# Half-row adds on GpSimd, and whole-load row sums, in a log-sum-exp kernel

## The chip, the cores and the metric

The kernel runs on one core of one Trainium2 chip. The metric is the device time of one execution in microseconds; "before" stands at a median of 162.42 us over 3 runs (162.29 to 162.43). The engines that matter are ScalarE (ACT, exponentials and logarithms), VectorE (DVE, sums), GpSimd (POOL), SyncE (SP, whose queue issues the transfers) and the 16 DMA engines. TensorE (PE) only adds up a check.

## The reference

For each of 32 x 512 = 16384 rows of 1024 float32 values, the reference gives one float32:

```python
max_x = np.max(x, axis=-1, keepdims=True)
return max_x.squeeze(-1) + np.log(np.sum(np.exp(x - max_x), axis=-1))
```

The input is drawn from a standard normal distribution, 67.1 MB in all, and each value is read once.

## The kernel before

**Tiling.** The rows are spread over 128 partitions, 128 rows per partition; a "row" below is one such column of 128 rows, 1024 values on each partition, and `c` counts them. Columns 0 to 111 (`W` = 112) and 112 to 127 are stored apart. The kernel takes exp(x) without subtracting the maximum, sums it, and takes the logarithm. A check of the sums (too small, too large, not a number) ends in one value, `fine`; only if it fails does a second pass with the maximum run, which does not happen with this input.

**Loads.** The list `LOADS` (L17) cuts the 128 rows into 18 transfers, numbered 0 to 17 here: sizes in rows, shrinking towards the end. SP issues all of them (L126) in that order into a ring of 48 rows in SBUF. A load that overwrites ring space waits first for whoever read it last (`users`, L119 to 126): SP's queue is in order, so a load that waits holds those behind it back. Load 3 starts again at ring row 0, and load 6 as well.

**What is done with a load** is written beside its size, one letter and a count of rows at a time. ScalarE waits for the landing once for the load, then works in place:

- `R`: one exponential over the rows (L192), then one VectorE row sum over them (L196).
- `T`: one exponential (L192), then for each row one VectorE instruction that adds the two halves of the row and sums the result (L204).
- `A`: ScalarE's exponential sums its row as it goes (L181); one row each.
- `Y`, `Z`: the two pieces of the last row, each summed by ScalarE (L170).

The last exponential of a load also covers what has landed of the row after.

**Order.** Each engine runs its instructions in the order in which this loop writes them. Waits between engines are counters (`Counted`), each wait naming how far another engine must have come. When `c` reaches `LATE` = 119, after the T3 of load 10, ScalarE gets the logarithm of columns 0 to 111 (L219), which waits for the VectorE instruction noted in `early_sum`, the last one that wrote these columns; VectorE gets the early check (L133, L138). After the loop come the store of these columns (L227), the logarithms of the remaining columns (L230, L232), their store (L236), the late check (L242) and `fine` (L251). GpSimd does nothing in the loop.

Of the kernel before, what the change touches and what calls it, by code (L numbers as in the profile page):

```python
# [13 lines left out]

LOADS = [  # L17
# [4 lines left out]
]  # L22


# [23 lines left out]
def kernel(  # L48
# [5 lines left out]
    nc = tc.nc  # L54
# [8 lines left out]
    AX = mybir.AxisListType  # L63
    ALU = mybir.AluOpType

    x_flat = x.flatten_outer_dims()
    n, d = x_flat.shape
    assert n % P == 0
    NC = n // P
    H = d // 2  # L70
    W = NC - B
# [7 lines left out]
    def source(e0, size):  # L79
        assert e0 >= W * d or e0 + size <= W * d  # L80
        return x_rest[:, e0 - W * d : e0 - W * d + size] if e0 >= W * d else x_rows[:, e0 : e0 + size]

    loads = [
        (int(size * d), [(op[0], 0 if op[0] == "Y" else int(op[1:] or 1)) for op in ops.split()])
        for size, ops in LOADS
    ]
# [3 lines left out]
    def sbuf(name, cols, dtype=fp32, rows=P):  # L90
        return nc.alloc_sbuf_tensor(name, [rows, cols], dtype).ap()

    ring = sbuf("ring", RING * d)
    sumexp = sbuf("sumexp", NC + 1)
# [10 lines left out]
    act = Counted(nc, nc.scalar, "act")  # L105
    dve = Counted(nc, nc.vector, "dve")
    pe = Counted(nc, nc.tensor, "pe")
    sp = Counted(nc, nc.sync, "early_store")
    done = nc.alloc_semaphore("done")
    again = nc.alloc_semaphore("again")  # L110
# [8 lines left out]
    users = []  # L119

    def load(i, here, done_before, size):
        for a, b, who, at in users:
            if a < here + size and b > here:
                sp.wait(who, at)
        users[:] = [u for u in users if not (u[0] < here + size and u[1] > here)]
        return nc.sync.dma_start(  # L126
            out=ring[:, here : here + size], in_=source(done_before, size)
        ).then_inc(landed[i], 16)

    def check_early():  # L130
        dve.wait(act, summed_by_act)
        dve.wait(dve, dve.n)
        dve.did(nc.vector.tensor_scalar(  # L133
            out=clamped[:, 0:LATE], in0=sumexp[:, 0:LATE],
            scalar1=LOW, scalar2=HIGH, op0=ALU.max, op1=ALU.min,
        ))
        dve.wait(dve, dve.n)
        dve.did(nc.vector.scalar_tensor_tensor(  # L138
            out=clamped[:, 0:LATE], in0=clamped[:, 0:LATE], scalar=0.0, in1=sumexp[:, 0:LATE],
            op0=ALU.bypass, op1=ALU.not_equal, accum_out=bad[:, 0:1],  # L140
        ))
        pe.wait(dve, dve.n)
        pe.did(nc.tensor.matmul(count, lhsT=bad[:, 0:1], rhs=far, start=True, stop=False))  # L143

    def add_up(c, who, **kw):
        pe.wait(*who)
        return pe.did(nc.tensor.matmul(count, lhsT=ones, rhs=sumexp[:, c : c + 1], **kw))  # L147

    c = 0
    p = 0  # L150
    here = 0
    done_before = 0
    summed_by_act = 0
    ln_early = None
    first_load = None
    for i, (size, ops) in enumerate(loads):
        if here + size > RING * d:
            assert here == p
            p = here = 0
        dma = load(i, here, done_before, size)  # L160
        first_load = first_load or dma.ins
        end = here + size
        done_before += size
        act.wait(landed[i], 16)
        for k, (how, s) in enumerate(ops):
            rows = ring[:, p : p + s * d].rearrange("p (c d) -> p c d", d=d)
            if how in "YZ":

                assert c == LAST and (how == "Z" or here == p)
                at = act.did(nc.scalar.activation(  # L170
                    out=last_exp[:, here - p : end - p], in_=ring[:, here:end], func=AF.Exp,
                    accum_out=sumexp[:, LAST : NC] if how == "Y" else sumexp[:, NC : NC + 1],
                ))
                here = end
                if how == "Y":
                    first_piece = at
                summed_by_act = at
            elif how == "A":
                assert here == p
                v = ring[:, p : p + d]  # L180
                at = act.did(nc.scalar.activation(  # L181
                    out=v, in_=v, func=AF.Exp, accum_out=sumexp[:, c : c + 1]
                ))
                here += d
                users.append((p, p + d, act, at))
                summed_by_act = at
                who = (act, at)
            else:

                upto = end if k + 1 == len(ops) and c + s < LAST else p + s * d  # L190
                v = ring[:, here:upto]
                at = act.did(nc.scalar.activation(out=v, in_=v, func=AF.Exp))  # L192
                here = upto
            if how == "R":
                dve.wait(act, at)
                who = (dve, dve.did(nc.vector.reduce_sum(  # L196
                    out=sumexp[:, c : c + s], in_=rows, axis=AX.X
                )))
                users.append((p, p + s * d, *who))
            elif how == "T":  # L200
                dve.wait(act, at)
                for r in range(s):
                    lo = rows[:, r, 0:H]
                    who = (dve, dve.did(nc.vector.scalar_tensor_tensor(  # L204
                        out=lo, in0=lo, scalar=1.0, in1=rows[:, r, H:d],
                        op0=ALU.mult, op1=ALU.add, accum_out=sumexp[:, c + r : c + r + 1],
                    )))
                    users.append((p + r * d, p + (r + 1) * d, *who))
                    if c + r >= LATE:
                        add_up(c + r, who, start=False, stop=False)  # L210
            if how == "A" and c >= LATE:
                add_up(c, who, start=False, stop=False)
            c += s
            p += s * d
            if c == LATE:

                act.wait(dve, early_sum)
                act.wait(act, early_act)
                ln_early = act.did(nc.scalar.activation(  # L219
                    out=res[:, 0:W], in_=sumexp[:, 0:W], func=AF.Ln  # L220
                ))
                check_early()
            if c <= W:
                early_sum, early_act = dve.n, summed_by_act
        assert here == end
    sp.wait(act, ln_early)
    nc.sync.dma_start(out=out_rows, in_=res[:, 0:W]).then_inc(sp.sem, 16)  # L227
# [5 lines left out]
        out=res[:, LAST:NC], in_=sumexp[:, NC : NC + 1], func=AF.Ln, bias=sumexp[:, LAST:NC]  # L233
# [9 lines left out]
        out=clamped[:, LATE:NC], in0=sumexp[:, LATE:NC], scalar=LOW,  # L243
        in1=sumexp[:, LATE:NC], op0=ALU.max, op1=ALU.not_equal, accum_out=bad[:, 1:2],
# [4 lines left out]
    at = add_up(NC, (act, summed_by_act), start=False, stop=True)  # L249
    dve.wait(pe, at)  # L250
    at = dve.did(nc.vector.tensor_scalar(out=fine, in0=count, scalar1=HIGH, scalar2=None, op0=ALU.is_lt))  # L251
# [6 lines left out]
    with nc.If(all_fine < 1):  # L258
# [3 lines left out]
        rows = 0  # L262
        steps = 0
        for c0 in range(0, NC, RING):
            s = min(RING, NC - c0)
# [5 lines left out]
            for c1, c2 in ((c0, edge), (edge, c0 + s)):  # L271
                if c1 == c2:
                    continue
                nc.scalar.dma_start(
                    out=ring[:, (c1 - c0) * d : (c2 - c0) * d],
                    in_=source(c1 * d, (c2 - c1) * d),
# [4 lines left out]
                out=neg, in_=v, op=ALU.max, axis=AX.X, negate=True  # L281
# [3 lines left out]
                out=v, in0=v, in1=neg[:, :, None].to_broadcast([P, s, d])  # L285
# [5 lines left out]
                out=sumexp[:, c0 : c0 + s], in_=v, axis=AX.X  # L291
# [71 lines left out]
```

## Time and profile before

| what | value |
|---|---|
| median of 3 runs | 162.42 us |
| the profiled execution, its own time | 162.54 us |
| its span, first to last instruction | 161.2 us |
| VectorE busy | 120.4 us (75%) |
| ScalarE busy | 116.2 us (72%) |
| GpSimd busy | 0.2 us (four memsets before the loop) |
| read from HBM | 67.11 MB, 417 GB/s over the span |
| transfers of the loads | 97.3% of the 16 DMA engines' span |
| VectorE's row sums, `R` | 15 instructions, 108.8 us |
| VectorE's half-row add and sum, `T` | 17 instructions, 10.7 us |
| ScalarE's summing exponentials, `A` | 9 instructions, 9.4 us |

The profile is of one execution; all places in time are microseconds from the start of its span. A busy share is an average: which engine sets the time is read stage by stage. A transfer has an issue on SP's queue and a time from issue to landing. When several transfers are queued, the time to landing includes the wait behind those ahead. An instruction on one engine can begin slightly before the one ahead has ended in the records, so durations in a row add up to a little more than the stretch they take: exponentials start some 0.09 us, row sums 0.08 us before the one ahead ends.

### The profile page before, as it was taken

Reading aid. Unit: us, or ns where it says so; the run is one execution under the profiler, and the core shown is the slowest. Engines: PE = TensorE matmul, PEld = TensorE weight load, DVE = VectorE, ACT = ScalarE, POOL = GpSimd, SP = SyncE. Lnnn points to the kernel's source line nnn. Section 1 sums busy time; section 2 is a strip of 40 time slices with the busy share of each in tenths; the row PEclk is TensorE's granted clock in tenths of the full one; section 3 lists DMA queues with packets and bytes.
Section 4 is the critical chain, followed back from the end, with each engine's and each line's share of the span. In section 5 each row is a group of like instructions: output and inputs, shape, how many; then the busy total and the mean of one; then the engine's idle time right before and its main releaser. Section 6 shows DMA issues by size and latency. Waiting matters only on the chain.

```text
span 161.2 us, 227 instructions
## 1 busy us (share of the span) xinstructions
PE 2.1 (1%) x24; PEld 1.0 (1%) x24; DVE 120.4 (75%) x57; ACT 116.2 (72%) x49; POOL 0.2 (0%) x4
## 2 busy tenths in 40 slices
PE   0000000000000000000000000000000000000022
PEld 0000000000000000000000000000000000000011
DVE  0000000009999999999999999999999995999894
ACT  3000059990799709995199949983999999989995
POOL 0000000000000000000000000000000000000000
DMA  7996996996996996996999999997999999999991
GB/s 260 520 520 276 504 520 276 504 520 276 504 520 276 504 520 276 504 520 276 463 439 439 439 423 407 445 534 331 439 439 419 434 407 430 442 419 410 410 397 25
DMA packets 2883, 67.19 MB, mean 417 GB/s; under 512 B 577, under 2 KB 705, under 8 KB 1345
## 3 DMA queue, kind: packets, MB, share of 16 engines
q1 hardware_dynamic: 2880, 67.18, 97.3%
q14 instruction: 3, 0.02, 0.0%
HBM read 67.11 MB, written 0.07 MB: 417 GB/s over the span
## 4 chain that ended last, share of the span: by engine, by line
DVE 51%; DMA 29%; ACT 16%; issue 2%; PE 0%
DVE sumexp L196 51%; DMA ring<-in_x_dram 29%; ACT ring L192 15%; ACT last_exp L170 1%; ACT res L219 0%; PE count L147 0%; DVE fine L251 0%
## 5 line engine op out<-in xcount | busy, mean ns | idle before, releaser
L196 DVE TENSOR_REDUCE sumexp<-ring 128x8 f32<-128x8192 f32 (+6 forms) x15 | 108.8, 7326 | 36.3 <-ACT ring L192 36.3
L192 ACT ACTIVATE ring<-ring 128x8192 f32<-128x8192 f32 (+15 forms) x23 | 103.8, 4571 | 41.8 <-DMA ring<-in_x_dram 41.8
L204 DVE SCALAR_TENSOR_TENSOR ring<-ring 128x512 f32<-128x512 f32 x17 | 10.7, 689 | 0.6 <-ACT ring L192 0.6
L181 ACT ACTIVATE ring<-ring 128x1024 f32<-128x1024 f32 x9 | 9.4, 1041 | 0.0
L114 ACT ACT_TABLE_LOAD x1 | 1.3, 1283 | 1.5 <-PEq L57 1.5
L143 PE MATMUL count<-far,bad 128*1 128x1 f32 x2 | 0.2, 164 | 153.7 <-DVE clamped L138 153.7
L147 PE MATMUL count<-sumexp,ones 128*1 128x1 f32 x20 | 1.8, 164 | 3.5 <-DVE ring L204 3.4
L181 ACT ACTIVATION_READ_ACCUMULATOR ring<-ring 128x1 f32 x9 | 1.7, 186 | 0.0
L204 DVE DVE_READ_ACCUMULATOR ring<-ring 128x1 f32 x17 | 1.4, 83 | 0.0
L115 DVE MEMSET ones<- 128x1 f32 x1 | 0.1, 59 | 1.5 <-PEq L57 1.5
L170 ACT ACTIVATE last_exp<-ring 128x640 f32<-128x640 f32 (+1 forms) x2 | 1.2, 591 | 0.0
L143 PEld LDWEIGHTS count<-far,bad 128*1 128x1 f32 x2 | 0.1, 80 | 153.7 <-DVE clamped L138 153.7
L147 PEld LDWEIGHTS count<-sumexp,ones 128*1 128x1 f32 x20 | 0.8, 81 | 4.4 <-DVE ring L204 4.2
L251 DVE TENSOR_SCALAR fine<-count 1x1 int32<-1x1 f32 x1 | 0.1, 147 | 0.6 <-PE count L147 0.6
L170 ACT ACTIVATION_READ_ACCUMULATOR last_exp<-ring 128x1 f32 x2 | 0.4, 186 | 0.0
L138 DVE SCALAR_TENSOR_TENSOR clamped<-clamped,sumexp 128x119 f32<-128x119 f32 x1 | 0.3, 284 | 0.0
L232 ACT ACTIVATE res<-sumexp 128x1 f32<-128x1 f32 x1 | 0.3, 294 | 0.0
L219 ACT ACTIVATE res<-sumexp 128x112 f32<-128x112 f32 x1 | 0.3, 279 | 0.0
L242 DVE SCALAR_TENSOR_TENSOR clamped<-sumexp 128x9 f32<-128x9 f32 x1 | 0.2, 169 | 0.1
L133 DVE TENSOR_SCALAR clamped<-sumexp 128x119 f32<-128x119 f32 x1 | 0.2, 222 | 0.0
L230 ACT ACTIVATE res<-sumexp 128x15 f32<-128x15 f32 x1 | 0.2, 198 | 0.0
L248 PE MATMUL count<-far,bad 128*1 128x1 f32 x2 | 0.2, 164 | 0.0
(8 smaller groups left out, 0.7 us busy)
## 6 DMA issues: line engine op xcount, KB each, us to landing
ring<-in_x_dram SPq DMA_DIRECT2D x1, 6912.0 KB, 26.0
ring<-in_x_dram SPq DMA_DIRECT2D x1, 6400.0 KB, 23.9
ring<-in_x_dram SPq DMA_DIRECT2D x1, 4608.0 KB, 17.7
ring<-in_x_dram SPq DMA_DIRECT2D x1, 3840.0 KB, 19.3
ring<-in_x_dram SPq DMA_DIRECT2D x1, 2816.0 KB, 25.6
ring<-in_x_dram SPq DMA_DIRECT2D x1, 2368.0 KB, 25.2
ring<-in_x_dram SPq DMA_DIRECT2D x1, 1696.0 KB, 21.7
ring<-in_x_dram SPq DMA_DIRECT2D x1, 1248.0 KB, 24.4
```

The costliest lines, as they stand in the source:

```text
L114: nc.scalar.preload_act_table_set("natural_log_exp_and_others")
L133: dve.did(nc.vector.tensor_scalar(out=clamped[:, 0:LATE], in0=sumexp[:, 0:LATE], scalar1=LOW, scalar2=HIGH, op0=ALU.max, op1=ALU.min,))
L138: dve.did(nc.vector.scalar_tensor_tensor(out=clamped[:, 0:LATE], in0=clamped[:, 0:LATE], scalar=0.0, in1=sumexp[:, 0:LATE], op0=ALU.bypass ...
L143: pe.did(nc.tensor.matmul(count, lhsT=bad[:, 0:1], rhs=far, start=True, stop=False))
L147: return pe.did(nc.tensor.matmul(count, lhsT=ones, rhs=sumexp[:, c : c + 1], **kw))
L170: at = act.did(nc.scalar.activation(out=last_exp[:, here - p : end - p], in_=ring[:, here:end], func=AF.Exp, accum_out=sumexp[:, LAST : NC ...
L181: at = act.did(nc.scalar.activation(out=v, in_=v, func=AF.Exp, accum_out=sumexp[:, c : c + 1]))
L192: at = act.did(nc.scalar.activation(out=v, in_=v, func=AF.Exp))
L196: who = (dve, dve.did(nc.vector.reduce_sum(out=sumexp[:, c : c + s], in_=rows, axis=AX.X)))
L204: who = (dve, dve.did(nc.vector.scalar_tensor_tensor(out=lo, in0=lo, scalar=1.0, in1=rows[:, r, H:d], op0=ALU.mult, op1=ALU.add, accum_out ...
L219: ln_early = act.did(nc.scalar.activation(out=res[:, 0:W], in_=sumexp[:, 0:W], func=AF.Ln))
L232: ln_last = act.did(nc.scalar.activation(out=res[:, LAST:NC], in_=sumexp[:, NC : NC + 1], func=AF.Ln, bias=sumexp[:, LAST:NC]))
```

## The change

A new letter, `F`: one exponential over the rows as in `R`; then GpSimd adds the second half of each row onto its first half, one `tensor_tensor` for all rows of the piece; then VectorE sums the half rows, one row sum over 512 values per row. VectorE's part is not written at once: it is kept in `folded`, and `reduce_folded` writes it when the next `F` begins, after the VectorE work of the next `R` or `T`, or before a load that would overwrite the rows. 35 rows are done this way, in seven pieces of 9, 6, 6, 4, 4, 3 and 3 rows in loads 3 to 8. No row is summed by ScalarE's `A` any more. Loads 1 and 2 are one piece of 16 rows each, as load 0 was (before: two of 8). Sizes and order of the loads, and loads 9 to 17, are as they were. In load 4 the piece that VectorE sums whole is now the second. Of the 35 rows, 29 were `R` before, 4 were `A` and 2 were `T`; the other five `A` rows become `R`.

```diff
 LOADS = [
-    (16, "R16"), (16, "R8 R8"), (16, "R8 R8"), (16, "R8 R8"), (13.5, "R7 R6"),
-    (12.5, "R7 R6"), (9, "A A A A A A A A A"), (7.5, "R3 R2 R2"), (5.5, "R4 T2"),
-    (4.625, "T4"), (3.3125, "T3"), (2.4375, "T3"), (1.8125, "T2"), (1.3125, "T1"), (0.9375, "T1"),
-    (0.5625, "T1"), (0.625, "Y"), (0.375, "Z"),
+    (16, "R16"), (16, "R16"), (16, "R16"), (16, "F9 R7"), (13.5, "F6 R7"), (12.5, "R7 F6"),
+    (9, "R5 F4"), (7.5, "F4 R3"), (5.5, "F3 F3"), (4.625, "T4"), (3.3125, "T3"), (2.4375, "T3"),
+    (1.8125, "T2"), (1.3125, "T1"), (0.9375, "T1"), (0.5625, "T1"), (0.625, "Y"), (0.375, "Z"),
 ]
...
+    folded = []
+
+    def reduce_folded():
+
+        nonlocal early_sum
+        while folded:
+            c0, s0, p0, n0 = folded.pop(0)
+            halves = ring[:, p0 : p0 + s0 * d].rearrange("p (c d) -> p c d", d=d)[:, :, 0:H]
+            dve.wait(pool, n0)
+            at = dve.did(nc.vector.reduce_sum(
+                out=sumexp[:, c0 : c0 + s0], in_=halves, axis=AX.X
+            ))
+            users.append((p0, p0 + s0 * d, dve, at))
+            if c0 < W:
+                early_sum = at
+
...
+        if any(q < here + size and q + t * d > here for _, t, q, _ in folded):
+            reduce_folded()
         dma = load(i, here, done_before, size)
...
-            if how == "R":
+            if how == "F":
+                reduce_folded()
+                pool.wait(act, at)
+                at = pool.did(nc.gpsimd.tensor_tensor(
+                    out=rows[:, :, 0:H], in0=rows[:, :, 0:H], in1=rows[:, :, H:d], op=ALU.add
+                ))
+                folded.append((c, s, p, at))
+            elif how == "R":
...
+            if how in "RT":
+                if c < W:
+                    early_sum = dve.n
+                reduce_folded()
             c += s
             p += s * d
             if c == LATE:
...
             if c <= W:
-                early_sum, early_act = dve.n, summed_by_act
+                early_act = summed_by_act
```

More of the change, by code (lines that the diff above doesn't have):

```diff
@@ L107 @@
     pe = Counted(nc, nc.tensor, "pe")
+    pool = Counted(nc, nc.gpsimd, "pool")
     sp = Counted(nc, nc.sync, "early_store")
@@ L151 @@
     here = 0
+    early_sum = 0
     done_before = 0
```

## The prediction

> **What bounds the kernel now.** Loads are numbered 0 to 17 in the order of the list; one "row" is 1024 values per partition. I read the chain that ended last first, since it names the work that sets the end. In start, length, work:
>
> ```profile
> 35.98 82.78 DVE sumexp L196 x9
> 118.76 0.02 issue
> 118.78 25.18 DMA ring<-in_x_dram
> 143.96 0.02 issue
> 143.98 4.08 ACT ring L192
> 148.07 2.91 issue
> 150.98 0.28 ACT res L219
> 151.26 6.50 ACT ring L192 x5
> 157.77 1.34 ACT last_exp L170 x4
> ```
>
> It blames VectorE's row sums for half the span. That is only who freed ring space last: the transfer issued at 118.78 is load 9, and it took 25.18 us to land because others were queued ahead of it. So I read the stretches next, in start:end, length, five busy engines, clock, DMA share, GB/s:
>
> ```profile
> 22.09:41.40 19.31, 0.00 (x0) 0.00 (x0) 5.42 (x1) 13.86 (x1) 0.00 (x0) 1.00 1.00 434
> 96.50:111.60 15.10, 0.00 (x0) 0.00 (x0) 15.10 (x2) 11.79 (x2) 0.00 (x0) 1.00 0.97 419
> 122.50:131.50 9.00, 0.00 (x0) 0.00 (x0) 9.00 (x2) 9.00 (x18) 0.00 (x0) 1.00 1.02 438
> ```
>
> The DMA engines are full whether VectorE is a quarter busy or wholly busy. Issue plus time to landing gives the landings: 22.07, 41.4, 60.76, 80.1, 96.5, 111.55, 122.53, 131.6, 138.3, 143.98 (load 9), 148.0, 151.07, 153.25, 154.92, 156.16, 156.9, 157.6, 158.2. From load 3 to load 9 that is 63.85 us for 52.625 rows; at load 1's 19.35 us for 16 rows it would be 63.65. The stream has no hole worth having. Third, ScalarE and VectorE in order of time near the end:
>
> ```profile
> 143.98 7.09 ACT L192 ACTIVATE ring<-ring 128x4736 f32<-128x4736 f32 x2 [0.43 <-DMA ring<-in_x_dram]
> 150.98 0.28 ACT L219 ACTIVATE res<-sumexp 128x112 f32<-128x112 f32 x1
> 151.17 6.60 ACT L192 ACTIVATE ring<-ring 128x2496 f32<-128x2496 f32 x5
> 157.77 0.71 ACT L170 ACTIVATE last_exp<-ring 128x640 f32<-128x640 f32 x1
> 150.01 0.69 DVE L204 SCALAR_TENSOR_TENSOR ring<-ring 128x512 f32<-128x512 f32 x1
> 151.10 0.69 DVE L204 SCALAR_TENSOR_TENSOR ring<-ring 128x512 f32<-128x512 f32 x1 [0.40 <-ACT ring L192]
> ```
>
> At 143.98 ScalarE still waits for a transfer; from there it never stops. Its exponentials start at 151.17, 153.35, 155.0, 156.2, 157.1, 157.77, 158.50 against landings at 151.07, 153.25, 154.92, 156.16, 156.9, 157.6, 158.2: always 0.1 to 0.3 us behind, never catching up. Whatever delays ScalarE or VectorE after 148 is paid at the end; what is saved before 143.98 is not.
>
> **The change, part by part.** The sizes, from the groups kept apart by shape (busy, mean ns):
>
> ```profile
> L196 DVE TENSOR_REDUCE sumexp<-ring 128x4 f32<-128x4096 f32 x1 | 4.4, 4409 | 0.0
> L196 DVE TENSOR_REDUCE sumexp<-ring 128x2 f32<-128x2048 f32 x2 | 4.5, 2276 | 0.0
> L347 POOL MEMSET const-float32-1.0<- 128x1 f32 x1 | 0.1, 99 | 0.0
> L115 DVE MEMSET ones<- 128x1 f32 x1 | 0.1, 59 | 1.5 <-PEq L57 1.5
> ```
>
> The sums give (4409-2276)/2048 = 1.0415 ns per value and 143 ns fixed, so half sums of 9, 6, 4, 3 rows take 4.94, 3.34, 2.28, 1.74 us. Exponentials not in the trace lie between their neighbours, 7021 ns for 8192 and 6176 for 7168 values for instance, 0.825 ns each. A handover between engines takes 0.02 us (35.96 to 35.98 in the chain).
>
> The half sums read 512 values and skip 512. No row sum here does, so three half rows lie between 1.74 and the 3.35 us of three whole rows. I take 1.74: the two-input add of `T` also reads half rows, at 1.20 ns a result, near the sums' rate.
>
> *GpSimd's add* is not in this trace. Fast end: VectorE's two-input add starts every 0.615 us for 512 results, 1.20 ns each. GpSimd's one-column float memset takes 99 ns against VectorE's 59, a ratio of 1.67; I take 2.0 ns per result as the nearest, and as the slow end the ratio once for each operand, 3.35 ns. Nothing else stands on GpSimd's queue. The Trainium skill (GPSIMD Engine Reference, Performance versus the Vector engine) has 4.497 us for 2048 such results, an estimate of 2.20 ns each; by it the sum below is the same.
>
> *Whole loads 1 and 2.* Row sums now wait for whole exponentials: 41.42+13.86 = 55.28, sum to 72.5; 60.78+13.86 = 74.64, sum (17.22) to 91.9. Load 4 is issued at 72.6 instead of 70.48, load 5 at 92.0 instead of 87.65. Load 0 landed 22.07 after issue for 19.35 us of data, so an issue keeps the stream full if it comes 2.72 us before the landing ahead of it: by 77.4 and 93.8. Price nothing; margin 1.8 us.
>
> *Load 3, "F9 R7".* Exponentials 7.87 and 6.18 from 80.1 end at 88.0 and 94.1. GpSimd adds 4608 results in 9.2 us, to 97.2. VectorE sums R7 to 101.7, the halves to 106.6. Load 6 goes out at 106.7 (104.83 before), due 108.8.
>
> *Load 4, "F6 R7".* R7 now comes second: exponentials 5.31+6.60 end at 108.3, R7's sum (7.61) at 115.9, the halves (3.34) at 119.2; GpSimd's adds, from 101.8, are done at 108. Loads 7 and 8, behind each other on SP's queue, both need these rows: 119.3 instead of 112.31, due 122.53-2.72 = 119.8. Price nothing, but by 0.5 us only; load 9 follows at 120.0, with load 8 already queued.
>
> *Load 5, "R7 F6".* R7 summed at 126.7 frees loads 10 to 13 (126.30 before). The halves wait behind load 6's R5, at 135.7; loads 14 to 17 go out from 135.8 (132.76 to 134.10 before), for landings after 156. Even with the last issue's 5.39 us again, hidden by 14 us.
>
> *Load 6, "R5 F4" for nine summed rows.* ScalarE: nine starts 1.04 us apart, 9.38 us, become 4.47+3.61, to 130.5 instead of 131.9. The 1.4 us saved become a longer wait for load 9, which lands at 143.98 as before. Worth nothing.
>
> *Load 7 and 8, "F4 R3", "F3 F3".* Exponentials end at 135.2, 138.3, 140.6, 143.2. GpSimd from load 5's rows on, at 2.0 ns: 122.5 to 128.7, 130.5 to 134.6, 135.2 to 139.3, 140.6 to 143.7, 143.7 to 146.8. VectorE is through with the first F3 by 145.5 and idles until load 9's exponential ends at 148.13; the two adds of load 8's T2 (1.23 us) that it no longer does only lengthen that idle time.
>
> *The last F3 and the early logarithm.* This is where time goes. In VectorE's program the last F3's half sum stands behind load 9's T4. T4 runs 148.15 to 150.6 as now; then 1.74 us for the half sum, to 152.39. The logarithm of the first 112 columns (L219) must read these three columns and stands on ScalarE ahead of the exponentials of loads 11 to 17. It ran at 150.98, its inputs long summed; now it starts at 152.40: +1.42. (With 3.35 us for the half sum it would be +3.03, 165.45.) Behind it queue five exponentials, Y, Z, both last logarithms and the last store, each +1.42 since ScalarE never had slack. VectorE: T3 of load 10 from 152.4 to 154.25, the early check (0.57) to 154.85, then load 11's exponential ends at 154.87; its last sum ends at 159.9, before Z's at 160.4. ScalarE sets the end. The early store moves from 151.28 to 152.7; it took 7.2 us, landing before the last store does.
>
> The Trainium skill (SBUF — State Buffer, Who interferes with whom) says that a VectorE instruction with two SBUF inputs and a GpSimd instruction reading SBUF exclude each other, while a tensor_reduce excludes nobody. By that rule only T4 could meet a GpSimd add here, which nothing in this trace can show; at its 2.20 ns the adds end by 147.4, before T4, and the sum stays.
>
> Sum: 1.42 us. The profiled execution took 162.54 (span 161.2 and 1.34 around it), so 163.96; it stands 0.12 above the median of 162.42, hence 163.84 there.
>
> **Rivals.**
> (a) *GpSimd is late.* From 122.5 it has 10240 results to add; past (150.6-122.5)/10240 = 2.74 ns the half sum waits for GpSimd instead of T4. At 3.0 the add ends at 153.25: +4.05, 166.5; at the slow end 156.8: +7.6, 170.0. Against: the ratio of the memsets. For: no row shows the operation.
> (b) *T4 waits for GpSimd,* if VectorE's two-input adds cannot run beside GpSimd's: from (148.13-122.5)/10240 = 2.5 ns the adds reach into T4, and T4, the half sum and everything behind shift, at 2.74 ns by 2.5 us more: 166.3. For and against: no GpSimd add runs beside a VectorE add in this trace. The Trainium skill's SBUF page, cited above, states this rule.
> (c) *The stream runs dry at load 7.* VectorE need only be 0.5 us later at 119.3. Every landing after moves by the excess: 0.3 to 1.0 us more, 164.1 to 164.8.
> (d) *The end is set by the transfers.* If ScalarE could go through loads 11 to 17 at least 1.4 us faster than they land, the late logarithm is absorbed, and with the stream's 0.2 us and the tail's 0.45 us (14.2 against 13.75 for 11.375 rows) the time would be 161.8 to 162.4. Against: its lag behind the landings never shrinks in the rows above.
>
> **How the numbers follow.** Forecast 0.70, own range 163.6 to 164.2; (a) 0.08; (b) 0.05; (c) 0.07; (d) 0.10, of which 0.06 faster and 0.04 within 0.2%, about what a measurement of this kernel can tell. Slower: 0.90. From 163.2 to 165.8 the range holds the forecast, (c), and about half of (a) and (b).
>
> **What would show it.** The logarithm near 152.4 with VectorE's half sum as releaser; a wait of 1.3 us on ScalarE before it where there was none; load 9 landing near 144.0; GpSimd's last add ending before 148; ScalarE's Z near 159.9. Wrong if load 9 lands after 144.3, if GpSimd's adds start further than 2.5 ns per result apart, or if the exponentials after the logarithm catch up with the landings.

## The result, and the profile after

The changed kernel takes 163.37 us in the median of 6 runs (163.3 to 164.05), the kernel before 162.42 (6 runs, 162.29 to 162.48): a ratio of the means of 1.0067, 95% interval 1.005 to 1.0083: slower by less than 1%, but clear of the noise. The profiled execution of the changed kernel took 163.32 us for a span of 162.0, 0.78 more than the one of before. VectorE is busy 112.8 us instead of 120.4, ScalarE 114.6 instead of 116.2, GpSimd 39.5 instead of 0.2: both busy engines have less to do, and the kernel is slower.

The end of the chain that ended last, after (start, length, work):

```profile
119.72 24.00 DMA ring<-in_x_dram
143.72 0.02 issue
143.75 4.16 ACT ring L212
147.90 0.02 issue
147.93 2.54 DVE ring L231 x8
150.47 1.68 DVE sumexp L159
152.14 0.02 issue
152.16 0.30 ACT res L250
```

Load 9 lands at 143.72 (143.98 before). Its exponential and T4's adds follow it as before (T4 begins 4.2 us behind the landing in both). Then comes a new link: the half sum of the last F3 (L159) and, behind it, the early logarithm (L250). ScalarE and VectorE in order of time around it:

```profile
143.75 7.08 ACT L212 ACTIVATE ring<-ring 128x4736 f32<-128x4736 f32 x2 [0.76 <-DMA ring<-in_x_dram]
152.16 0.30 ACT L250 ACTIVATE res<-sumexp 128x112 f32<-128x112 f32 x1 [1.33 <-DVE sumexp L159]
152.37 6.59 ACT L212 ACTIVATE ring<-ring 128x2496 f32<-128x2496 f32 x5
158.86 0.69 ACT L190 ACTIVATE last_exp<-ring 128x640 f32<-128x640 f32 x1
147.93 0.69 DVE L231 SCALAR_TENSOR_TENSOR ring<-ring 128x512 f32<-128x512 f32 x1 [2.29 <-ACT ring L212]
150.38 1.75 DVE L159 TENSOR_REDUCE sumexp<-ring 128x3 f32<-128x1536 f32 x1
```

ScalarE stops for 1.33 us in a stretch in which it never stopped before, and the work behind runs back to back again. VectorE, which idled 2.29 us before T4, has the half sum only after T4.

The logarithm stood 7.00 us behind load 9's landing (150.98-143.98) and stands 8.44 behind it (152.16-143.72): +1.44 us. From the logarithm to the check on VectorE it is 8.30 us instead of 8.40 (160.46-152.16, 159.38-150.98), -0.10. The landing itself is 0.26 earlier, and the last store lands 1.4 us after its issue instead of 1.7, -0.3. Sum: 1.44-0.10-0.26-0.3 = 0.78, the difference of the two executions.

GpSimd's adds, which no row of before showed, by shape (busy, mean ns):

```profile
L217 POOL TENSOR_TENSOR ring<-ring 128x3072 f32<-128x3072 f32 x2 | 13.4, 6718 | 17.9 <-ACT ring L212 17.9
L217 POOL TENSOR_TENSOR ring<-ring 128x2048 f32<-128x2048 f32 x2 | 9.1, 4536 | 1.4 <-ACT ring L212 1.4
```

and the last two in order of time:

```profile
140.41 6.85 POOL L217 TENSOR_TENSOR ring<-ring 128x1536 f32<-128x1536 f32 x2 [0.89 <-ACT ring L212]
```

That is 2.19 and 2.21 ns per result (2.16 to 2.24 over all seven adds), and the last one ends at 147.26, 0.67 us before T4 begins.

### The profile page after: what moved, and what is told of

The parts are those of the page before. It is cut to its first block, busy times and chain, and to the rows that moved or that the text cites. A ratio compares the mean times of both kernels' runs of the same rounds, so it can differ in the third digit from the quotient of the medians.

```text
span 162.0 us, 209 instructions
## 1 busy us (share of the span) xinstructions
PE 2.1 (1%) x24; PEld 1.0 (1%) x24; DVE 112.8 (70%) x53; ACT 114.6 (71%) x30; POOL 39.5 (24%) x11
## 4 chain that ended last, share of the span: by engine, by line
DMA 54%; DVE 23%; ACT 20%; SPq 0%; issue 0%; PE 0%; DVEq 0%
DMA ring<-in_x_dram 54%; ACT ring L212 20%; DVE sumexp L223 15%; DVE ring L231 5%; DVE sumexp L159 3%; SPq L127 0%; ACT res L250 0%; PE count L279 0%; DVE clamped L273 0%; PE count L148 0%; DVE fine L282 0%; DVEq L44 0%
## 5 line engine op out<-in xcount | busy, mean ns | idle before, releaser
L212 ACT ACTIVATE ring<-ring 128x16384 f32<-128x16384 f32 (+17 forms) x22 | 111.6, 5121 | 43.1 <-DMA ring<-in_x_dram 43.1
L223 DVE TENSOR_REDUCE sumexp<-ring 128x16 f32<-128x16384 f32 (+3 forms) x8 | 83.3, 10419 | 42.9 <-ACT ring L212 42.9
L217 POOL TENSOR_TENSOR ring<-ring 128x3072 f32<-128x3072 f32 (+3 forms) x7 | 39.3, 5621 | 107.5 <-ACT ring L212 107.5
L159 DVE TENSOR_REDUCE sumexp<-ring 128x6 f32<-128x3072 f32 (+3 forms) x7 | 19.6, 2812 | 0.3 <-POOL ring L217 0.3
L231 DVE SCALAR_TENSOR_TENSOR ring<-ring 128x512 f32<-128x512 f32 x15 | 9.5, 686 | 2.4 <-ACT ring L212 2.3
L250 ACT ACTIVATE res<-sumexp 128x112 f32<-128x112 f32 x1 | 0.3, 297 | 1.3 <-DVE sumexp L159 1.3
```

The lines of the kernel that those rows point to most:

```text
L159: at = dve.did(nc.vector.reduce_sum(out=sumexp[:, c0 : c0 + s0], in_=halves, axis=AX.X))
L217: at = pool.did(nc.gpsimd.tensor_tensor(out=rows[:, :, 0:H], in0=rows[:, :, 0:H], in1=rows[:, :, H:d], op=ALU.add))
L223: who = (dve, dve.did(nc.vector.reduce_sum(out=sumexp[:, c : c + s], in_=rows, axis=AX.X)))
L231: who = (dve, dve.did(nc.vector.scalar_tensor_tensor(out=lo, in0=lo, scalar=1.0, in1=rows[:, r, H:d], op0=ALU.mult, op1=ALU.add, accum_out ...
L250: ln_early = act.did(nc.scalar.activation(out=res[:, 0:W], in_=sumexp[:, 0:W], func=AF.Ln))
```

## Experiments

Times are medians, with the kernel before run on the same chip beside each (162.40 to 162.48). Ratios are of the means, to that kernel.

**1. Load 8 as before.** On the changed kernel:

```diff
-    (9, "R5 F4"), (7.5, "F4 R3"), (5.5, "F3 F3"), (4.625, "T4"), ...
+    (9, "R5 F4"), (7.5, "F4 R3"), (5.5, "R4 T2"), (4.625, "T4"), ...
```

> The changed kernel with load 8 as before ("R4 T2" for "F3 F3"); the 29 half-added rows of loads 3 to 7 and the whole loads 1 and 2 stay. Theory (the last F3's half sum stands behind load 9's T4 and holds the early logarithm): the whole loss goes, 162.2 to 162.6 us, logarithm straight behind load 10's exponential near 151. Rival (GpSimd running beside VectorE, or the later issues, cost the time): 163.2 to 163.5, nearly unchanged.

163.19 us (9 runs, 162.91 to 164.75), ratio 1.0058 [1.0034, 1.0082]: the time missed what the theory said, the places did not. The logarithm is back, directly behind load 10's exponential, and the last store is issued at 159.51, against 159.45 before and 160.53 in the changed kernel:

```profile
150.81 0.28 ACT L250 ACTIVATE res<-sumexp 128x112 f32<-128x112 f32 x1
151.00 6.59 ACT L212 ACTIVATE ring<-ring 128x2496 f32<-128x2496 f32 x5
159.51 0.34 SPq L267 DMA_DIRECT2D out_dram<-res  x1
```

Its last store in the list of transfers (issues, KB, us to landing):

```profile
out_dram<-res SPq DMA_DIRECT2D x1, 8.0 KB, 2.4
```

Of the 1 us that the compute gained, the last store gives back most: the same 8 KB took 2.4 us to land, 1.4 in the changed kernel. I ran it once more to see whether that was chance.

> The kernel with load 8 as before, once more, for its last store: it took 2.4 us to land there, 1.4 to 1.7 us elsewhere. If that belongs to the kernel: 2.2 us or more and 163.0 us or more again. If it was that execution's: 1.4 to 1.7 us and 162.1 to 162.5.

163.13 us in one run, and the store took 2.2 us. So it seems to belong to this program. In both executions nine of the store's 144 packets come 0.2 to 0.4 us behind the others, directly after one packet of 8 KB on another queue (of the kind "instruction" in the list of transfers) that starts among them. In the profiles whose store takes 1.4 us such a packet comes only 0.2 to 0.7 us after the landing. That the store waits for it is argued and not tried, and it does not explain the 1.7 us of before, where no packet of the store is late. So this experiment shows the logarithm's place; the time itself is settled by experiment 2.

**2. The half sum ahead of T4.** All GpSimd work stays; only VectorE's order changes.

```diff
             elif how == "T":
+                reduce_folded()
                 dve.wait(act, at)
```

> The changed kernel, with the pending half sum written ahead of the adds of a T instead of behind them; all GpSimd work stays. Theory: GpSimd's last add ends at 147.3, the half sum then runs to 149.0 and T4 begins 0.9 us later than in the changed kernel, at 149.0; the logarithm is not held and stands near 151.0; VectorE's T3 of load 10 starts at 151.5 instead of 152.05 (151.10 before): 162.5 to 162.9 us. Rival (GpSimd's presence costs, not the order): 163.2 to 163.5. Rival (what counts is the 1.74 us of VectorE work wherever it stands): 163.1 to 163.4.

162.41 us (12 runs, 162.29 to 163.67), ratio 1.0006 [0.9993, 1.002]: the whole loss is gone, 0.1 us below my range.

```profile
147.34 1.75 DVE L159 TENSOR_REDUCE sumexp<-ring 128x3 f32<-128x1536 f32 x1 [1.65 <-POOL ring L217]
149.01 0.68 DVE L232 SCALAR_TENSOR_TENSOR ring<-ring 128x512 f32<-128x512 f32 x1
150.70 0.28 ACT L251 ACTIVATE res<-sumexp 128x112 f32<-128x112 f32 x1
```

The half sum now even waits 1.65 us for GpSimd and T4 begins 1.1 us later than in the changed kernel. But the logarithm is not held. VectorE's last sum then ends about where ScalarE's end is, so its own lateness costs little: from ScalarE's start on load 9 to the issue of the last store it is 15.62 us (143.69 to 159.31), against 15.47 before and 16.78 in the changed kernel. The 0.15 us that are left are hidden by the store, which lands in 1.4 us here as in the changed kernel, and in 1.7 before. Neither GpSimd's presence nor VectorE's amount of work is the price; the place of one instruction is.

**3. Only the hold on ScalarE removed.** VectorE's order is that of the changed kernel; the logarithm stands behind load 11's exponential.

```diff
             if c == LATE:
-
+                check_early()
+            if c == LATE + 3:
                 act.wait(dve, early_sum)
...
                 ))
-                check_early()
```

> The changed kernel, with the early logarithm one exponential later on ScalarE, behind load 11's; VectorE's order unchanged. Theory: ScalarE is no longer held, its exponentials follow the landings again, but VectorE's own queue is still one half sum late, with its last sum ending near 159.5 instead of 159.7; the time is then VectorE's: 162.7 to 163.0 us. If the hold on ScalarE were the whole price: 162.3 to 162.5. If it were none of it: 163.3.

162.96 us (6 runs, 162.87 to 163.06), ratio 1.003 [1.0018, 1.0042]: 0.56 us of the 0.95 are left, inside the theory's range.

```profile
158.37 0.47 ACT L190 ACTIVATE last_exp<-ring 128x384 f32<-128x384 f32 x1
159.57 0.22 ACT L261 ACTIVATE res<-sumexp 128x15 f32<-128x15 f32 x1 [0.61 <-DVE ring L231]
```

ScalarE's Z is back to 158.37 and then waits 0.61 us for VectorE's last sum. The late half sum acts twice: through the logarithm on ScalarE, and through VectorE's own queue, which holds the last logarithms to 159.57, against 159.01 before.

**4. The last half sum ahead of T4 by the list alone.**

```diff
-    ... (5.5, "F3 F3"), ...
+    ... (5.5, "F4 R2"), ...
```

> The changed kernel with load 8 as "F4 R2" instead of "F3 F3": one row more on GpSimd, but the last half sum stands behind R2, ahead of load 9's T4. Theory: GpSimd's add ends at 145.7, R2 and the half sum end at 148.0, T4 and the logarithm stand where they stood before the change: 162.3 to 162.5 us. Rival (half sums so close to the end cost wherever they stand): 163 or more.

162.22 us in the median, but from 161.9 to 163.74 (12 runs; ratio 1.0006 [0.9982, 1.003]): eight of them at most 162.26, four at 163.0 and above. The typical run confirms the theory: VectorE's half sum runs 145.96 to 148.25, T4 from 148.17, the logarithm at 150.77. The scatter stands out here, and experiments 6 to 8 look for its cause.

**5. Load 6 as before.**

```diff
-    (9, "R5 F4"), ...
+    (9, "A A A A A A A A A"), ...
```

> The changed kernel with load 6 as before, nine rows summed by ScalarE, in place of "R5 F4". Theory: the 1.3 us that ScalarE saves in load 6 only lengthen its waits for loads 7 and 9, so the time stays at that of the changed kernel, 163.2 to 163.5 us. Rival (the saved ScalarE time was worth something at the end): 163.7 to 164.7.

163.54 us (4 runs, 163.28 to 164.27), ratio 1.0078 [1.0056, 1.01], 0.04 above the theory's range, beside 163.37 of the changed kernel (163.3 to 164.05). The ranges overlap. What ScalarE saves in load 6 is worth nothing that these runs can tell.

**6. Whole loads alone.** On the kernel before:

```diff
-    (16, "R16"), (16, "R8 R8"), (16, "R8 R8"), (16, "R8 R8"), ...
+    (16, "R16"), (16, "R16"), (16, "R16"), (16, "R8 R8"), ...
```

> The kernel before, with loads 1 and 2 in one exponential and one row sum each and nothing else. Theory: nothing, 162.3 to 162.5 us; loads 4 and 5 are issued near 72.2 and 91.6 with the stream full. Rival (the later issues cost part of the loss): 162.6 or more.

164.31 us (5 runs, 164.05 to 165.12), ratio 1.0117 [1.0101, 1.0134]: a clear miss. Twice VectorE waits 2.1 us for a whole exponential; with load 3 still in two row sums of 8 it then has them done only at 109.1, so load 6 is issued 4.3 us later than before.

```profile
74.63 62.38 DVE L196 TENSOR_REDUCE sumexp<-ring 128x16 f32<-128x16384 f32 x7 [2.13 <-ACT ring L192]
125.45 1.06 ACT L181 ACTIVATE ring<-ring 128x1024 f32<-128x1024 f32 x1 [2.93 <-DMA ring<-in_x_dram]
```

Load 6 in its list of transfers:

```profile
ring<-in_x_dram SPq DMA_DIRECT2D x1, 4608.0 KB, 16.3
```

ScalarE starts on load 5 at 111.56 and on load 6 at 125.45, each 0.02 us behind the landing: 13.9 us apart instead of 10.9 (111.61 and 122.53 before) for load 6's 9 rows. So 3.0 us of the stream are lost, nearly all of them a wait of ScalarE. The issue, at 109.12, came 2.4 us ahead of the landing before it (the 2.46 and 2.9 in the next expectation come from a time to landing that the view rounds to 0.1 us). The profiled execution, 165.12 us, is the slowest of the five; the median lost 1.9 us against before. In the changed kernel "F9 R7" takes 4.5 rows of summing off VectorE in load 3, load 6 goes out at 106.27, and nothing is lost.

**7. Loads 7 and 8 issued 0.6 us later.** One more VectorE instruction ahead of load 4's half sums, on the changed kernel:

```diff
+            if c0 == 64:
+                dve.did(nc.vector.reduce_sum(
+                    out=clamped[:, LAST:NC], in_=ring[:, 42 * d : 42 * d + 512], axis=AX.X
+                ))
             dve.wait(pool, n0)
```

> The changed kernel, with one more VectorE row sum over 512 values (its result is not used) ahead of load 4's half sums, so that loads 7 and 8 are issued 0.6 us later, 2.7 us before load 6 lands instead of 3.3. Theory (an issue 2.72 us ahead keeps the stream full, and what is missing is lost one for one): 163.3 to 163.5 us. Rival (the limit lies between 2.46 us, where the whole loads alone lost 2.9 us, and 3.3, and a miss costs more than it is late): 164 to 166.5.

164.47 us (4 runs, 163.3 to 165.21), ratio 1.0118 [1.0079, 1.0157]. In its profile, of an execution of 164.25 us, load 7 is issued at 119.61, 2.7 us before load 6 lands at 122.33, and lands 10.0 us after it instead of 9.1. The issue line of load 7 first in the changed kernel, then here, and then ScalarE's wait for it here, in order of time:

```profile
ring<-in_x_dram SPq DMA_DIRECT2D x1, 3840.0 KB, 12.4
```

```profile
ring<-in_x_dram SPq DMA_DIRECT2D x1, 3840.0 KB, 12.7
```

```profile
132.31 11.68 ACT L216 ACTIVATE ring<-ring 128x4096 f32<-128x4096 f32 x4 [1.98 <-DMA ring<-in_x_dram]
```

0.9 us lost with an issue 2.7 us ahead, none with 3.3 us: in the profiles the limit lies between, and the changed kernel stands close to it. It is not sharp: of the four times here, one (163.3) shows no loss.

**8. Load 4 with R7 first.** The kernel of experiment 4, with one pair swapped back:

```diff
-    ... (13.5, "F6 R7"), ...
+    ... (13.5, "R7 F6"), ...
```

> The kernel of "F4 R2" in load 8, with load 4 as "R7 F6" instead of "F6 R7": loads 7 and 8 are then issued near 114, 8 us before load 6 lands instead of 3.3. Theory (with 3.3 us the stream sometimes runs dry at load 7, which is where a third of that kernel's times stood over 1 us above the others): median 161.9 to 162.2 us and no time above 162.6. Rival (the scatter has another cause): times above 163 among them again, median near 162.2.

162.17 us (9 runs, 161.99 to 162.27), ratio 0.9978 [0.9968, 0.9988]. Load 7 is issued at 114.15, 8.4 us before load 6 lands, and no time is high any more. The runs with and without the lead show that the scatter goes with it. Single times 0.7 to 1.6 us above the median also stand in the changed kernel (one of 6) and in experiments 1 (two of 9), 2 (one of 12) and 5 (one of 4), all with 3.3 us at load 7; experiments 3 and 9 (10 runs) have none. With 8.4 us there is none in 20 runs, the next kernel's included. That the stream ran dry in just those executions was not seen: no profile is of one of them. It is faster than the kernel before by 0.2%, but hardly through the change: its last store is issued at 159.47 (159.45 before) and lands in 1.4 us instead of 1.7.

> As the kernel with load 4's R7 first, with loads 1 and 2 again in two pieces of 8 rows. Theory: both have issue leads of more than 3.5 us at every load, so the same 161.9 to 162.2 us and no time above 162.6. Rival (whole loads leave too little lead at load 5 or 6): faster than the kernel with whole loads by 0.2 us or more, or free of high times where that one has them.

With loads 1 and 2 back in pieces of 8 (`(16, "R8 R8"), (16, "R8 R8")` in that list): 162.22 us (11 runs, 162.1 to 162.38), ratio 0.9981 [0.9972, 0.999]. The same; with the lead there, whole loads cost nothing.

**9. GpSimd beside the T adds.** On the changed kernel, after the last GpSimd add:

```diff
+        if i == 8:
+            pool.wait(dve, third_summed)
+            for spare in (6, 4):
+                pool.wait(pool, pool.n)
+                v = ring[:, 42 * d : (42 + spare) * d].rearrange("p (c d) -> p c d", d=d)
+                pool.did(nc.gpsimd.tensor_tensor(
+                    out=v[:, :, 0:H], in0=v[:, :, 0:H], in1=v[:, :, H:d], op=ALU.add
+                ))
```

> The changed kernel, with two more GpSimd adds (6 and 4 rows, 3072 and 2048 results, on rows of the ring that are no longer needed; their results are not used) behind its last one, from 147.3 to 158.5 beside VectorE's T adds. If VectorE's two-input adds exclude GpSimd's: T4 waits for GpSimd or GpSimd for it, T adds take longer than their 0.69 us or begin late, 165 us or more. If the two run side by side: T adds 0.69 us as before, 163.3 to 163.5. In between (they slow each other): T adds 0.75 to 1.2 us, 164 to 168.

173.88 us (4 runs), ratio 1.0704 [1.0689, 1.072].

```profile
147.56 11.58 POOL L264 TENSOR_TENSOR ring<-ring 128x3072 f32<-128x3072 f32 x2
147.99 6.80 DVE L231 SCALAR_TENSOR_TENSOR ring<-ring 128x512 f32<-128x512 f32 x1 [2.19 <-ACT ring L212]
154.72 4.97 DVE L231 SCALAR_TENSOR_TENSOR ring<-ring 128x512 f32<-128x512 f32 x1
159.62 0.68 DVE L231 SCALAR_TENSOR_TENSOR ring<-ring 128x512 f32<-128x512 f32 x1
```

A T add that takes 0.68 us alone takes 6.80 beside GpSimd's first added instruction, the next 4.97 beside its second: each lasts until GpSimd's add is over and a little more. GpSimd itself loses little (6.68 us for 3072 results instead of 6.72, 4.82 for 2048 instead of 4.54). VectorE's row sums, by contrast, go on: in the changed kernel the two R7 of loads 3 and 5, half covered by GpSimd adds, take 7.62 and 7.61 us, the R7 of before 7.61. So a two-input add on VectorE waits for a whole GpSimd add, and a row sum does not. In the changed kernel GpSimd is done 0.67 us before T4, so this cost nothing there.

## Why the prediction was right, and where it was off

**What bounds.** Right. Load 9 lands at 143.72, ScalarE is idle before it (0.76 us, 0.43 before), and all savings ahead of it vanish.

**The last F3 and the early logarithm.** Right in place and size: +1.42 forecast, +1.44 measured against load 9's landing, with the half sum at 1.75 us (1.74 forecast). Experiment 2 removes it by order alone; experiment 3 shows both ways it acts.

**The sum** was 0.5 us too large, 163.84 against 163.37. The median lies 0.2 us below the forecast's own range (163.6 to 164.2) and inside the wide one, whose lower end of 163.2 was margin and not worked out from a term. The mis-sized terms stand behind the logarithm: I carried the shift unchanged to the end. In the profiles the tail from there was 0.10 us shorter. I had read ScalarE as always 0.1 to 0.3 us behind the landings and never catching up; in the trace of before the exponentials of loads 12 to 14 and Y start only 0.02 to 0.05 us behind theirs, so they still waited, and that slack took up 0.1 us. It is all that is left of rival (d): after the late logarithm no exponential waited for a landing. And the last store landed 0.3 us sooner after its issue. With both, 1.42 becomes 1.02, beside 0.95 between the medians. The stream's 0.26 differs from execution to execution (load 0 lands from 21.7 to 22.1 us in the profiles) and says nothing about the change. The prediction had treated the store's landing as part of a fixed rest; it is 1.4, 1.7 or 2.2 to 2.4 us for the same 8 KB. Where it falls was chance for this forecast: with the 2.4 us of experiment 1 the time would have been some 164.4, above the sum.

**GpSimd's add.** 2.0 ns per result taken, 2.16 to 2.24 measured. The Trainium skill (GPSIMD Engine Reference, Performance versus the Vector engine) has 4.497 us for 2048 results; the row here has 4.536. Rival (a) needed 2.74 ns.

**Half sums** with gaps cost what contiguous ones cost (1.75 us for 1536 values); the slow end of 3.35 us falls.

**Rival (b)** is a true mechanism with no part in this result. The Trainium skill's rule (SBUF — State Buffer, Who interferes with whom) agrees with experiment 9: 6.80 us instead of 0.68. It misses this kernel by 0.67 us.

**The issues of loads 4 to 9.** The places came out to 0.5 us (load 7 at 118.87, 119.3 forecast; load 6 at 106.27, 106.7), most of it because load 0 landed 0.38 us earlier in this execution; but the due times were wrong. I took load 0's excess, 2.72 us, as the lead that an issue needs; experiments 6 and 7 lose 3.0 us at 2.4 and 0.9 us at 2.7. The margin at load 7 that I put at 0.5 us was less, and in some executions perhaps none. And the price of rival (c), "the excess", was too low: at load 6 of experiment 6 the excess by that rule was 0.3 us and 3.0 were lost.

**"Whole loads: price nothing"** holds beside "F9 R7" and not by itself. That step was worked out in the schedule of the changed kernel; my expectation for experiment 6 copied the result to a schedule in which load 6 goes out at 109.1, though 108.8 was its due time by my own rule. What that expectation said of loads 4 and 5 came out (72.53 and 91.88, stream full); it stopped one load too early.

## What to carry to other kernels

When a deferred instruction is written "after the next piece of work", look at who reads its result and what queues behind that reader: 1.75 us of VectorE work, put one place too late, cost 0.95 us, and 7.6 us of saved VectorE work brought in nothing, because the stream of transfers set the time there. In a kernel that is bound by a full stream of transfers, follow every issue's lead over the landing before it; parts of a change that are free together can lose microseconds alone. Before moving work to GpSimd, list the two-input VectorE instructions that can meet it.

## What was not expected of the hardware

- An issue 2.7 us ahead of the running transfer's landing lost 0.9 us of the stream and one 2.4 us ahead 3.0 us; 3.3 us lost none in the profiles. The loss is not one for one.
- A VectorE two-input add of 0.68 us took 6.80 us beside a GpSimd add, a whole instruction's wait and not a slower pace.
- The same last store of 8 KB landed in 1.4, 1.7 or 2.2 to 2.4 us, nearly the same for one program in two executions (2.4 and 2.2); why stays open, and at this kernel's end it is worth as much as the change.
